# Two of the five and a half gate/up pairs of each feed-forward part as seven block products instead of eight

## The chip, the cores and the metric

The kernel runs on one core of one Trainium2 chip. The time is that of one launch on the device in microseconds (us): the median of three runs before the change is 1303.59 us, and the three lie between 1303.38 and 1304.42 us. A profile shows one execution of the same program; its times count from that execution's first instruction.

## The reference

The program is a two-layer decoder trunk over 256 tokens of width 1024, in float32. Each layer has a feed-forward part, a token mixer (differential attention in layer 0, a Mamba-2 mixer in layer 1), a cross-attention into 256 memory tokens, and a second feed-forward part. There are four feed-forward parts in all, and they are what the change touches.

```python
def swiglu(h, w_gate, w_up, w_down):
    return (jax.nn.silu(h @ w_gate) * (h @ w_up)) @ w_down
...
    h = h + 0.5 * swiglu(rmsnorm(h, ffn1_norm[i]), ffn1_w_gate[i], ffn1_w_up[i], ffn1_w_down[i])
```

Here `w_gate` and `w_up` are 1024 x 2816, and `w_down` is 2816 x 1024. The norm's root is a factor per token; it is applied after the gate/up products, its gains before them.

## The kernel before

**Tiles.** The 256 tokens are two row tiles of 128 (t = 0, 1). Width 1024 is eight tiles of 128 rows (kt = 0 to 7). The hidden width 2816 is five chunks of 512 (c = 0 to 4) and one of 256 (c = 5); a chunk of gate and of up is called a pair here. The normed activations lie transposed in `norm.x` as eight pairs of tiles (`xh`, `xl`).

**Precision by three products.** Each float32 operand is split into a high part that TensorE takes exactly and the low rest. `mm3` (L220) issues three matmuls per block: high by high (L221), high by low (L222, `wlo`) and low by high (L223, `xl`). All write 512 columns of one bank of PSUM; there are eight banks (pool `pacc`).

**Weights.** A `W` (L145) is one 1 MB tile (4 kt by 512 columns) that SP loads from device memory into pool `wp`, which has 4 buffers. A granule, `Gran` (L164), is half of it (2 kt by 512). Its `split` (L171) casts the high part on ScalarE (`whi`, L183) and subtracts on VectorE (`wlo`, L184), into pool `hp` with 4 buffers of each. `use` (L196) writes the split of a granule three granules ahead of the matmuls that take it. A cast can start when TensorE has finished the granule four places earlier, since that frees its buffer.

**A feed-forward part.** `ffn_hidden` (L572) runs `wide` (L248) over the chunks: gate 0, up 0, gate 1, up 1, and so on, each with 4 granules of 12 matmuls (2 kt x 2 row tiles x 3). After gate, ScalarE takes the silu (L581); after up, VectorE multiplies (L598); then eight transposes (`htp`, L611) and another split (L614, L615) make four of the 22 hidden tiles. Down is `out_b` (L276): half 0 of the output columns over all 22 hidden tiles, then half 1, 11 granules each. In the last part `last` does this with its own order, in which row tile 1 of half 1 goes in two pieces of 256 columns (`fin`).

**What sets the order.** The program is written with a clock of its own (`Pipe`, L108): `pipe.pe` adds the time of the matmuls written so far, and `pipe.after` puts side work (evacuations, transposes) at a later time on that clock. The scheduler of the compiler keeps that as a priority and may move an instruction on its engine when it holds it to be ready earlier. Each engine then runs its own list strictly in order.

## Time and profile before

| | |
|---|---|
| median of three runs | 1303.59 us |
| span of the profiled execution (first to last instruction) | 1301.7 us |
| TensorE (PE) busy | 1293.3 us, 99% |
| VectorE (DVE) busy | 826.3 us, 63% |
| ScalarE (ACT) busy | 716.0 us, 55% |
| GpSimd (POOL) busy | 73.1 us, 6% |
| mean rate of the DMA queues | 178 GB/s |
| granted TensorE clock, mean | 0.998 |

The profiled execution's own time is known only by its span; the median of the runs lies 1.9 us above it. In the rows, a number such as L184 is a line of the kernel before. "out<-in" names the tile that is written and those that are read. "x402 | 498.5, 1242" is the count, the busy time in us and the mean duration of one in ns. What stands behind a second bar or in brackets is the time for which the engine sat idle just before, and what ended it.

### The profile page before, as it was taken

To read this page: it belongs to the slowest core of one execution; us is meant where nothing else is said; L and a number is where in the kernel's file an instruction comes from. 1 tells how busy PE (TensorE), PEld (TensorE's weight loads), DVE (VectorE), ACT (ScalarE), POOL (GpSimd) and SP (SyncE) were. 2 spreads that over 40 slices of the span, in tenths; PEclk is the share of its full clock that TensorE was granted. 3 is DMA by queue.
4 is the path that set the end of the run, shared out by engine and by line. 5 is a ranking of instruction groups with operands and counts; after the bars stand their busy time and mean duration, and the time that the engine had idled before them with its cause. 6 is when DMAs were issued, how large, how long until landed. Compare 5 with 4: busy or idle time off the path is not lost.

```text
span 1301.7 us, 17808 instructions
## 1 busy us (share of the span) xinstructions
PE 1293.3 (99%) x6997; PEld 1112.6 (85%) x6997; DVE 826.3 (63%) x1211; ACT 716.0 (55%) x1176; POOL 73.1 (6%) x67
## 2 busy tenths in 40 slices
PE   9999999999999999999999999999999999999998
PEld 7888888788988888888888889999998998888887
DVE  5656457876666555555556446798897775655554
ACT  6456444685455545444445446677865664544432
POOL 1000002200000000000000000022132000000000
PEclk9999999999999999999999999999999999999999
DMA  9565555434445553656554655665634445655551
GB/s 329 179 220 183 188 180 193 131 129 165 161 160 162 188 190 124 226 181 212 182 186 150 211 193 185 205 195 162 195 130 168 163 157 161 208 172 172 206 178 49
DMA packets 138726, 232.01 MB, mean 178 GB/s; under 512 B 5737, under 2 KB 42258, under 8 KB 138642
## 3 DMA queue, kind: packets, MB, share of 16 engines
q1 hardware_dynamic: 137744, 229.75, 53.5%
q8 instruction: 55, 0.90, 0.3%
q10 hardware_dynamic: 738, 0.59, 0.1%
q0 software_dynamic: 160, 0.52, 0.1%
q14 instruction: 29, 0.24, 0.1%
HBM read 229.77 MB, written 1.08 MB: 177 GB/s over the span
## 4 chain that ended last, share of the span: by engine, by line
PE 96%; DVE 2%; DMA 1%; ACT 1%; issue 0%; POOL 0%; SPq 0%; POOLq 0%; ACTq 0%
PE out L221 7%; PE out L223 7%; PE out L222 7%; PE up L222 6%; PE up L223 6%; PE up L221 6%; PE gate L221 5%; PE gate L223 5%; PE gate L222 5%; PE xs L221 1%; PE htp L611 1%; PE xs L223 1%; PE xs L222 1%; PE fin L221 1%; PE fin L222 1%; PE fin L223 1%
## 5 line engine op out<-in xcount | busy, mean ns | idle before, releaser
L184 DVE TENSOR_TENSOR wlo<-w,whi 128x1024 fp32r<-128x1024 f32 (+2 forms) x446 | 526.4, 1186 | 399.6 <-ACT whi L183 398.0
L183 ACT CAST whi<-w 128x1024 fp32r<-128x1024 f32 (+1 forms) x448 | 447.6, 1006 | 463.9 <-PE out L223 141.4
L222 PE MATMUL up<-wlo,xh 128*128 128x512 f32 x320 | 124.6, 389 | 0.1
L223 PE MATMUL up<-whi,xl 128*128 128x512 f32 x320 | 124.5, 389 | 0.0
L221 PE MATMUL up<-whi,xh 128*128 128x512 f32 x320 | 124.5, 389 | 0.0
L221 PE MATMUL gate<-whi,xh 128*128 128x512 f32 x312 | 123.3, 395 | 0.0
L223 PE MATMUL gate<-whi,xl 128*128 128x512 f32 x312 | 121.7, 390 | 0.0
L222 PE MATMUL gate<-wlo,xh 128*128 128x512 f32 x312 | 121.6, 390 | 0.0
L221 PE MATMUL out<-whi,hid_hi 128*128 128x512 f32 x264 | 103.5, 392 | 0.0
L223 PE MATMUL out<-whi,hid_lo 128*128 128x512 f32 x264 | 102.8, 389 | 0.0
L222 PE MATMUL out<-wlo,hid_hi 128*128 128x512 f32 x264 | 102.7, 389 | 0.0
L222 PEld LDWEIGHTS up<-wlo,xh 128*128 128x128 f32 x320 | 60.1, 188 | 12.9 <-DVE wlo L184 0.5
L221 PEld LDWEIGHTS up<-whi,xh 128*128 128x128 f32 x320 | 60.1, 188 | 12.5
L223 PEld LDWEIGHTS up<-whi,xl 128*128 128x128 f32 x320 | 60.1, 188 | 12.5
L223 PEld LDWEIGHTS gate<-whi,xl 128*128 128x128 f32 x312 | 58.6, 188 | 12.3
L222 PEld LDWEIGHTS gate<-wlo,xh 128*128 128x128 f32 x312 | 58.7, 188 | 12.1 <-POOL wlo L184 0.4
L221 PEld LDWEIGHTS gate<-whi,xh 128*128 128x128 f32 x312 | 58.6, 188 | 11.5
L223 PEld LDWEIGHTS out<-whi,hid_lo 128*128 128x128 f32 x264 | 49.6, 188 | 10.4
L221 PEld LDWEIGHTS out<-whi,hid_hi 128*128 128x128 f32 x264 | 49.6, 188 | 10.1
L222 PEld LDWEIGHTS out<-wlo,hid_hi 128*128 128x128 f32 x264 | 49.6, 188 | 10.0
L315 POOL TENSOR_TENSOR rcol<-msq,neghalf 128x2 f32<-128x2 f32 x8 | 5.7, 718 | 683.4 <-DVE msq L313 683.4
L221 PE MATMUL fin<-whi,hid_hi 128*128 128x512 f32 (+1 forms) x110 | 38.3, 348 | 0.0
(355 smaller groups left out, 2729.9 us busy)
## 6 DMA issues: line engine op xcount, KB each, us to landing
w<-in_ffn_w_up_dram SPq DMA_DIRECT2D x40, 1024.0 KB, 5.1
w<-in_ffn_w_down_dram SPq DMA_DIRECT2D x40, 1024.0 KB, 5.2
w<-in_ffn_w_gate_dram SPq DMA_DIRECT2D x38, 1024.0 KB, 5.1
w<-in_ssd_w_in_dram SPq DMA_DIRECT2D x24, 1024.0 KB, 5.4
w<-in_xa_w_kv_dram SPq DMA_DIRECT2D x16, 1024.0 KB, 5.1
w<-in_da_w_in_dram SPq DMA_DIRECT2D x12, 1024.0 KB, 5.1
w<-in_xa_w_q_dram SPq DMA_DIRECT2D x8, 1024.0 KB, 5.1
w<-in_xa_w_o_dram SPq DMA_DIRECT2D x8, 1024.0 KB, 5.0
```

Of the source, the lines that this page charges most:

```text
L183: nc.scalar.copy(hv, src)
L184: self.eng.tensor_tensor(self.lo[:, :, o:o + n], src, hv.bitcast(F32), op=ALU.subtract)
L221: nc.tensor.matmul(o, lhsT=lh, rhs=rh, start=start, stop=False)
L222: nc.tensor.matmul(o, lhsT=lh, rhs=rl, start=False, stop=False)
L223: nc.tensor.matmul(o, lhsT=ll, rhs=rh, start=False, stop=stop)
L315: nc.gpsimd.tensor_tensor(c[:, :n], m[:, :n], neghalf[:, :n], op=ALU.pow)
L611: nc.tensor.transpose(tp[:, j, t * P:(t + 1) * P], us[t][:, (i + j) * P:(i + j + 1) * P], ident)
```

## The change

A pair is one product of a 2 x 2 by a 2 x 2 block matrix: the activations in blocks of row tile t by half h of the width (kt 0 to 3 and 4 to 7), the weights in blocks of half h by up or gate. Written out, that is eight block products of 4 kt each. For chunks 3 and 4 of each part, `seven` does it with seven products (a Strassen form) on sums of blocks:

- **Sums of activations.** `Norm.combine` adds `xh` and `xl` up to full tiles (`y`), forms four sums or differences (`sraw`), and splits them (`s_hi`, `s_lo`), once per part for both pairs. It is written to begin 8 us after the norm's last tile on the program's clock.
- **Sums of weights.** `Sum` makes x1 = b11 + b12 on VectorE into a buffer of its own; x2 = x1 + b22 and later x4 = x2 + b21 in the same buffer by DMAs that POOL issues, which read b22 and b21 once more from device memory and add them to what lies in SBUF; and x3 = b12 + b22 in place on VectorE.
- **The products.** Each product is two granules of 6 matmuls in one bank. `seven_fin` adds the seven banks up to two gate and two up tiles.
- **Order.** The 256-wide chunk comes third. Chunks 1 and 2 (the stream, 16 granules) then alternate with chunk 3's 14 granules, two and two, in a `weave`; chunk 4's 14 alternate with 14 granules of down (both halves over hidden tiles 0 to 11, 20 and 21). Half 1's partial sum is added to `h`; half 0's stays in its banks. Down then finishes over hidden tiles 12 to 19.
- **Buffers.** `wp` has 6 buffers, the small work tiles 9 for 10, and the DMA descriptors of POOL less space.

```diff
-    wp = ctx.enter_context(tc.tile_pool(name="wp", bufs=4))
+    wp = ctx.enter_context(tc.tile_pool(name="wp", bufs=6))
...
+    class Sum:
+        def __init__(self, l, r, into=None):
+            self.l, self.r, self.into, self.k0 = l, r, into, 0
+            self.t = None
+        def load(self):
+            if self.t is not None:
+                return
+            self.l.load()
+            if self.into is None:
+                self.r.load()
+                self.t = wp.tile([P, 2048], F32, name="w", tag="w").rearrange("p (k c) -> p k c", c=512)
+            else:
+                self.t = self.l.t
+            w = self.r
+            for k in (0, 2):
+                ks = slice(k, k + 2)
+                if self.into == "dma":
+                    r0 = (w.k0 + k) * P
+                    nc.gpsimd.dma_start(self.t[:, ks, :], w.src[r0:r0 + 2 * P, w.c0:w.c0 + w.n]
+                                        .rearrange("(k p) c -> p k c", p=P), accum_op=ALU.add)
+                else:
+                    nc.vector.tensor_tensor(self.t[:, ks, :], self.l.t[:, ks, :], w.t[:, ks, :], op=ALU.add)
...
+    def seven(src1, src2, c0, norm, after):
+        b11, b21 = (W(src1, k, 4, c0, 512) for k in (0, 4))
+        b12, b22 = (W(src2, k, 4, c0, 512) for k in (0, 4))
+        x1 = Sum(b11, b12)
+        x2 = Sum(x1, b22, "dma")
+        x4 = Sum(x2, b21, "dma")
+        x3 = Sum(b12, b22, "here")
+        banks = {}
+        def a(t, h):
+            return lambda k: tuple(x[:, t * P:(t + 1) * P] for x in pipe.need(norm.x, 4 * h + k))
+        def s(nm):
+            return lambda k: tuple(x[:, k * P:(k + 1) * P] for x in pipe.need(norm.s, nm))
+        plan = [(x1, s(0)), (b11, a(0, 0)), (b22, s(1)), (x2, s(2)), (b21, a(0, 1)), (x3, s(3)), (x4, a(1, 1))]
+        out = []
+        for i, (w, lhs) in enumerate(plan):
+            for k0 in (0, 2):
+                def step(g, i=i, lhs=lhs, k0=k0):
+                    if not k0:
+                        banks[i] = acc("seven")
+                    for k in range(k0, k0 + 2):
+                        lh, ll = lhs(k)
+                        mm3(banks[i], lh, ll, g.hi[:, k - k0, :], g.lo[:, k - k0, :], k == 0, k == 3)
+                        pipe.pe(0.68)
+                    if k0:
+                        if i in (0, 3):
+                            (x4 if i else x2).load()
+                        after(i, banks)
+                out.append((Gran(w.k0 + k0, 2, (w, 0, 512)), step))
+        return out
+    def weave(steps):
+        def run(*gr):
+            for g, (_, f) in zip(use(gr), steps):
+                f(g)
+        units.append(([g for g, _ in steps], run))
+    def down(src, half, ks, lhs, banks, first, last):
+        def step(g):
+            if not banks:
+                banks.extend(acc("out") for _ in range(2))
+            for k in range(g.nk):
+                kt = g.k0 + k
+                for t in range(2):
+                    xh, xl = pipe.need(lhs, kt)
+                    ts = slice(t * P, (t + 1) * P)
+                    mm3(banks[t], xh[:, ts], xl[:, ts], g.hi[:, k, :], g.lo[:, k, :], kt == first, kt == end)
+                    pipe.pe(0.68)
+                if kt == end:
+                    last(half, banks)
+        end = ks[-1][0] + ks[-1][1] - 1 if last else -1
+        return [(Gran(k, 2, (w, 0, 512)), step) for w in [W(src, k0, nk, half * 512, 512) for k0, nk in ks]
+                for k in range(w.k0, w.k0 + w.nk, 2)]
...
+            if self.mixes and len(self.x) == KT:
+                self.combine(8.0)
+        def combine(self, wait):
+            self.s = [None] * 4
+            y = [slot("y") for _ in range(4)]
+            raw = {}
+            def full(p):
+                for j in range(2):
+                    xh, xl = self.x[2 * p + j]
+                    nc.vector.tensor_tensor(v2(y[p])[:, j, :], xh.bitcast(F32), xl.bitcast(F32), op=ALU.add)
+            def part(t, h):
+                return [v2(y[2 * h + p])[:, :, t * P:(t + 1) * P] for p in range(2)]
+            def mix(i, l, r, op):
+                raw[i] = work("sraw")
+                o = raw[i].rearrange("p (h j t) -> p h j t", h=2, j=2)
+                l, r = (raw[x].rearrange("p (h j t) -> p h j t", h=2, j=2) if isinstance(x, int) else x for x in (l, r))
+                for p in range(2):
+                    lp, rp = (x[p] if isinstance(x, list) else x[:, p, :, :] for x in (l, r))
+                    nc.vector.tensor_tensor(o[:, p, :, :], lp, rp, op=op)
+            def cut(i):
+                hi, lo = slot("s_hi", F32R), slot("s_lo", F32R)
+                nc.scalar.copy(hi, raw[i])
+                nc.vector.tensor_tensor(lo, raw[i], hi.bitcast(F32), op=ALU.subtract)
+                self.s[i] = (hi, lo)
+            steps = [lambda p=p: full(p) for p in range(4)]
+            steps += [lambda: mix(0, part(1, 0), part(1, 1), ALU.subtract), lambda: cut(0),
+                     lambda: mix(2, 0, part(0, 0), ALU.subtract),
+                     lambda: mix(1, 2, part(0, 1), ALU.add), lambda: cut(1), lambda: cut(2),
+                     lambda: mix(3, part(0, 0), part(1, 0), ALU.subtract), lambda: cut(3)]
+            for i, f in enumerate(steps):
+                pipe.after(wait + 1.6 * i, f)
...
+        def seven_fin(c):
+            us, t = {}, {}
+            def after(i, b):
+                v = nc.vector
+                if i in (0, 1):
+                    t[i] = work(f"p{i}")
+                    pipe.after(0.7, lambda: nc.scalar.copy(t[i], b[i]))
+                def c12():
+                    t[3] = work("p3")
+                    v.tensor_tensor(t[3], b[3], t[1], op=ALU.add)
+                    v.tensor_tensor(t[0], t[0], t[3], op=ALU.subtract)
+                    us[0] = work("c12")
+                    v.tensor_tensor(us[0], b[2], t[0], op=ALU.add)
+                    nc.scalar.activation(us[0], us[0], AF.Silu, scale=norm.col[:, 0:1])
+                def up0():
+                    v.tensor_tensor(t[1], b[4], t[1], op=ALU.add)
+                    v.scalar_tensor_tensor(us[0], t[1], norm.col[:, 0:1], us[0], op0=ALU.mult, op1=ALU.mult)
+                def c22():
+                    us[1] = t[0]
+                    v.tensor_tensor(t[0], t[0], b[5], op=ALU.subtract)
+                    nc.scalar.activation(t[0], t[0], AF.Silu, scale=norm.col[:, 1:2])
+                    v.tensor_tensor(t[3], b[5], t[3], op=ALU.add)
+                def up1():
+                    v.tensor_tensor(t[3], b[6], t[3], op=ALU.add)
+                    v.scalar_tensor_tensor(us[1], t[3], norm.col[:, 1:2], us[1], op0=ALU.mult, op1=ALU.mult)
+                    pipe.after(T["hid"], lambda: turn(c, [us[0], us[1]], 512))
+                    extras(c)
+                if i in (3, 4, 5, 6):
+                    pipe.after(0.7, {3: c12, 4: up0, 5: c22, 6: up1}[i])
+            return after
...
         first = {} if units else dict(single=True, eng=nc.gpsimd)
-        for c in range(HID // 512):
-            wide([(wg, c * 512, 512)], norm, "gate", gate_fin(c), **first)
-            first = {}
-            wide([(wu, c * 512, 512)], norm, "up", up_fin(c))
+        wide([(wg, 0, 512)], norm, "gate", gate_fin(0), **first)
+        wide([(wu, 0, 512)], norm, "up", up_fin(0))
         c = HID // 512
         wide([(wg, c * 512, 256), (wu, c * 512, 256)], norm, "gateup", up_fin(c, 256, 256))
-        return hid
+        n = [x for c in (1, 2) for x in stream([(wg, c * 512, 512)], norm, "gate", gate_fin(c))
+             + stream([(wu, c * 512, 512)], norm, "up", up_fin(c))]
+        s = seven(wu, wg, 3 * 512, norm, seven_fin(3))
+        weave([x for i in range(0, 14, 2) for x in n[i:i + 2] + s[i:i + 2]] + n[14:])
+        s = seven(wu, wg, 4 * 512, norm, seven_fin(4))
+        wd = a[nm + "_w_down"][l]
+        banks = [], []
+        def part(half, ps):
+            def go():
+                for t in range(2):
+                    nc.vector.scalar_tensor_tensor(h[t][half], ps[t], 0.5, h[t][half], op0=ALU.mult, op1=ALU.add)
+            pipe.after(0.7, go)
+        ks = [(0, 4), (4, 4), (8, 4), (20, 2)]
+        d = down(wd, 1, ks, hid, banks[1], 0, part) + down(wd, 0, ks, hid, banks[0], 0, None)
+        weave([x for i in range(0, 14, 2) for x in s[i:i + 2] + d[i:i + 2]])
+        return hid, wd, banks[0]
     def ffn(nm, l, norm, nxt, extra=None):
-        hid = ffn_hidden(nm, l, norm, extra)
-        out_b(a[nm + "_w_down"][l], NHT, hid, upd(0.5, nxt))
+        hid, wd, bank = ffn_hidden(nm, l, norm, extra)
+        fin = upd(0.5, nxt)
+        ks = [(12, 4), (16, 4)]
+        weave(down(wd, 0, ks, hid, bank, 0, fin) + down(wd, 1, ks, hid, [], 12, fin))
...
-            cuts = [4, 4, 4, 4, 6] if half else [4, 4, 4, 4, 4, 2]
-            k0 = 0
-            for nk in cuts:
-                ws = {k: W(a["ffn2_w_down"][1], k, min(4, k0 + nk - k), half * 512, 512) for k in range(k0, k0 + nk, 4)}
+            k0 = 12
+            for nk in [2, 6] if half else [4, 4]:
+                ws = {k: W(wd, k, min(4, k0 + nk - k), half * 512, 512) for k in range(k0, k0 + nk, 4)}
...
```

The rest of the diff hands the part's state through (`hid` by index, `held` banks in `last`). What the change does to the order is shown at three places of the second feed-forward part of layer 0.

TensorE, before, where gate of a chunk gives way to its up (`gate`, `up`: the banks; `whi`, `wlo`: the split weights):

```order
L221 MATMUL gate<-whi,xh 128x512
L222 MATMUL gate<-wlo,xh 128x512
L223 MATMUL gate<-whi,xl 128x512
L221 MATMUL up<-whi,xh 128x512
L222 MATMUL up<-wlo,xh 128x512
L223 MATMUL up<-whi,xl 128x512
```

TensorE, changed, where the first product's second granule gives way to the next stream granule (`s_hi`, `s_lo`: a split sum of activations):

```order
L246 MATMUL seven<-whi,s_hi 128x512
L247 MATMUL seven<-wlo,s_hi 128x512
L248 MATMUL seven<-whi,s_lo 128x512
L246 MATMUL gate<-whi,xh 128x512
L247 MATMUL gate<-wlo,xh 128x512
L248 MATMUL gate<-whi,xl 128x512
```

Runs of 12 product matmuls now stand between runs of 24 stream matmuls, and each uses the same three-matmul block as before.

VectorE, before, at the first pairs of that part:

```order
L184 TENSOR_TENSOR wlo<-w,whi 128x1024 x7
L598 SCALAR_TENSOR_TENSOR gs<-up,rcol,gs 128x512 x2
L184 TENSOR_TENSOR wlo<-w,whi 128x1024 x2
L615 TENSOR_TENSOR hid_lo<-htp,hid_hi 128x512 x2
L184 TENSOR_TENSOR wlo<-w,whi 128x1024 x6
L598 SCALAR_TENSOR_TENSOR gs<-up,rcol,gs 128x512 x2
```

VectorE, changed, where the 256-wide chunk ends and the first weave begins (`w<-w`: the sums x1, then x3):

```order
L209 TENSOR_TENSOR wlo<-w,whi 128x2x256 x2
L187 TENSOR_TENSOR w<-w 128x1024 x2
L209 TENSOR_TENSOR wlo<-w,whi 128x1024
L794 TENSOR_TENSOR hid_lo<-htp,hid_hi 128x512 x2
L494 TENSOR_TENSOR s_lo<-sraw,s_hi 128x512
L209 TENSOR_TENSOR wlo<-w,whi 128x1024 x2
L738 SCALAR_TENSOR_TENSOR gs<-gateup,rcol,gs 128x256 x2
L209 TENSOR_TENSOR wlo<-w,whi 128x1024
L187 TENSOR_TENSOR w<-w 128x1024 x2
L794 TENSOR_TENSOR hid_lo<-htp,hid_hi 128x512
L209 TENSOR_TENSOR wlo<-w,whi 128x1024 x13
```

The sum x1 stands ahead of the weave's first split, and x3, which waits for b22, behind its fourth.

POOL, changed, over the second part of layer 0 and the first of layer 1 (each `w` row: the two halves of one accumulating DMA; before, the four `rcol` of these stages stood in one row):

```order
L416 TENSOR_TENSOR rcol<-msq,neghalf 128x2 x2
L184 DMA w<-in_ffn_w_gate_dram 128x2x512 x2
L184 DMA w<-in_ffn_w_up_dram 128x2x512 x2
L184 DMA w<-in_ffn_w_gate_dram 128x2x512 x2
L184 DMA w<-in_ffn_w_up_dram 128x2x512 x2
L416 TENSOR_TENSOR rcol<-msq,neghalf 128x2
```

Eight accumulating DMAs per part, two for each of four sums, now stand on POOL between the norms' small operations.

More of the change, by code (lines that the diff above doesn't have):

```diff
@@ L81, in work @@
     def work(name, n=512, dt=F32):
[L83 removed]
+        return wk.tile([P, n], dt, name=name, tag="v", bufs=9) if n <= 256 else wk.tile([P, n], dt, name=name, tag="w")
     ident = const.tile([P, P], F32, name="ident")
@@ L274, in wide, with stream @@
                             eng=eng if k in ((3, 5) if single else (6,)) else None) for k, nk in cut], run))
+    def stream(parts, norm, name, fin):
+        ws = [[W(src, k, 4, c0, n) for k in range(0, KT, 4)] for src, c0, n in parts]
+        ps = []
+        def step(g):
+            if not ps:
+                ps.extend(acc(name) for _ in range(2))
+            for k in range(g.nk):
+                kt = g.k0 + k
+                xh, xl = pipe.need(norm.x, kt)
+                for t in range(2):
+                    ts = slice(t * P, (t + 1) * P)
+                    mm3(ps[t], xh[:, ts], xl[:, ts], g.hi[:, k, :], g.lo[:, k, :], kt == 0, kt == KT - 1)
+                    pipe.pe(0.68)
+            if kt == KT - 1:
+                fin(ps)
+        return [(Gran(k, 2, *((w[k // 4], 0, n) for w, (_, _, n) in zip(ws, parts))), step) for k in (0, 2, 4, 6)]
@@ L1297, in run @@
                     if (t, c0) not in banks:
-                        banks[t, c0] = acc("fin")[:, :c1 - c0]
+                        banks[t, c0] = acc("fin")[:, :c1 - c0] if half else held[t]
                     b = banks[t, c0]
@@ L1302, in run @@
                             kt = g.k0 + k
-                            mms(b, t, g, k, slice(c0, c1), kt, kt == NHT - 1)
+                            mms(b, t, g, k, slice(c0, c1), kt, half == 1 and kt == 12, kt == 19)
                     if last_:
```

43 lines of the change are left out of this document (26 added, 17 removed).

## The prediction

> **What bounds the kernel now.** I read the head of the page first, then TensorE's own waits, the table of stretches, and single rows of the timeline for the pace of one matmul.
>
> ```profile
> span 1301.7 us, 17808 instructions
> PE 1293.3 (99%) x6997; PEld 1112.6 (85%) x6997; DVE 826.3 (63%) x1211; ACT 716.0 (55%) x1176; POOL 73.1 (6%) x67
> ```
>
> TensorE is busy in all but 8.4 us of the span. The waits that ended on it are few, and none lies in a feed-forward part:
>
> ```profile
> PE warm L398 <- DVE warm L99: 1.5, 1, 1.5
> PE acs L987 <- issue: 0.2, 1, 0.2
> PE qkt L673 <- POOL rt L664: 0.2, 1, 0.2
> ```
>
> One gate/up pair in the second part, and the last stretch of the span (columns: length, then busy us and count of PE, PEld, DVE, ACT, POOL, then clock, DMA share, GB/s):
>
> ```profile
> 434.00:456.66 22.66, 22.66 (x105) 18.84 (x104) 12.32 (x12) 10.76 (x12) 0.00 (x0) 1.00 0.59 187
> 1290.00:1301.70 11.70, 5.29 (x41) 4.93 (x39) 5.81 (x24) 1.82 (x4) 1.12 (x2) 0.82 0.28 91
> ```
>
> A pair keeps TensorE busy for all of 22.66 us at full clock, VectorE for 54% of it, ScalarE for 47%. Of the 8.4 idle us, 6.4 are the tail. So in the feed-forward parts the number of matmuls sets the time, and a matmul less is worth the distance from one start to the next:
>
> ```profile
> 58.67 0.39 PE L221 MATMUL gate<-whi,xh 128*128 128x512 f32 x1
> ...
> 64.79 0.39 PE L221 MATMUL gate<-whi,xh 128*128 128x512 f32 x1
> ...
> 65.25 0.39 PE L223 MATMUL gate<-whi,xl 128*128 128x512 f32 x1
> 65.47 0.39 PE L221 MATMUL up<-whi,xh 128*128 128x512 f32 x1
> ...
> 1266.98 0.28 PE L221 MATMUL fin<-whi,hid_hi 128*128 128x256 f32 x1
> ...
> 1268.89 0.28 PE L222 MATMUL fin<-wlo,hid_hi 128*128 128x256 f32 x1
> ```
>
> From 58.67 to 64.79 lie 27 starts: 0.2267 us each, not the 0.39 of one matmul's duration, which overlaps the next. The step from gate to up, into other banks, costs the same 0.22, so changing banks and operands every 6 or 12 matmuls is charged nothing. The 256-column form takes 1.91 / 16 = 0.119 us.
>
> The Trainium skill, "TensorE: Matmul & The Clock Gate", section "Back-to-back issue gap", gives a sustained roofline of about 131 ns per matmul of 512 columns. By that figure the 96 matmuls below would be worth 12.6 us; the row says 0.2267, and the row decides.
>
> **The change part by part.** *Matmuls removed.* A pair is 8 block products of 4 kt x 3 = 96 matmuls; seven make 84. Two pairs in each of four parts: 96 matmuls x 0.2267 = 21.8 us. In the last part 84 matmuls of 256 columns become 42 of 512: 84 x 0.119 - 42 x 0.2267 = 0.5 us. Transposes (176 `htp`) stay. Together 22.3 us off TensorE, which is on the path throughout.
>
> *Splits and sums added.* The durations:
>
> ```profile
> L184 DVE TENSOR_TENSOR wlo<-w,whi 128x1024 fp32r<-128x1024 f32 x402 | 498.5, 1242 | 380.8 <-ACT whi L183 379.3
> L183 ACT CAST whi<-w 128x1024 fp32r<-128x1024 f32 x402 | 421.7, 1052 | 443.9 <-PE out L223 141.4 <-PE up L223 90.0 <-PE gate L223 81.4
> L615 DVE TENSOR_TENSOR hid_lo<-htp,hid_hi 128x512 fp32r<-128x512 f32 x44 | 28.6, 683 | 3.1 <-ACT hid_hi L614 3.1
> L598 DVE SCALAR_TENSOR_TENSOR gs<-up,rcol,gs 128x512 f32<-128x512 f32 x40 | 28.2, 745 | 0.3
> L581 ACT ACTIVATE gs<-gate,rcol 128x512 f32<-128x512 f32 x40 | 27.2, 689 | 14.1 <-PE gate L223 14.0
> L614 ACT CAST hid_hi<-htp 128x512 fp32r<-128x512 f32 x44 | 24.0, 591 | 5.1 <-PE htp L611 3.5
> L1275 DVE TENSOR_TENSOR h<-h,fn 128x256 f32<-128x256 f32 x6 | 2.4, 421 | 0.0
> ```
>
> A pair had 8 granules; a seven has 14, so 48 more splits in all. I add up the first weave with its two trailing stream granules. TensorE: 16 x 12 x 0.2267 + 14 x 6 x 0.2267 + three sets of `htp` at 22.66 - 96 x 0.2267 = 0.9 each, 65.3 us. VectorE: 30 splits x 1.242 = 37.3; four weight sums of the same shape, 5.0; nine operations of `seven_fin`, 7 x 0.683 + 2 x 0.745 = 6.3; four up products, 3.0; six `hid_lo`, 4.1. That is 55.7 us, 85% of TensorE's time where it was 54%. ScalarE: 30 x 1.052 + 2 copies and 6 `hid_hi` x 0.591 + 6 silus x 0.689 = 40.4, 62%. On the sum VectorE still fits; it could hold TensorE up only where work bunches. A weight sum does so twice per weave.
>
> The steady rhythm of the kernel before shows the reserve:
>
> ```profile
> 548.04 1.05 ACT L183 CAST whi<-w 128x1024 fp32r<-128x1024 f32 x1 [1.67 <-PE out L223]
> 549.13 1.23 DVE L184 TENSOR_TENSOR wlo<-w,whi 128x1024 fp32r<-128x1024 f32 x1 [1.50 <-ACT whi L183]
> ```
>
> A cast starts when TensorE ends the granule four back, and `wlo` is done 2.3 us later (548.04 to 550.36). TensorE wants it after the three granules between: 3 x 2.72 = 8.2 us before, reserve 5.8. A seven granule lasts 6 x 0.2267 = 1.36, so three in a row last 5.4 us at least (two of 1.36, one of 2.72), reserve 3.1, about two more operations of 1.24 on VectorE.
>
> *The tight place: x3.* x3's sum stands on VectorE behind the weave's fourth split, and needs b22. Six buffers hold the sum, b11, b12 and three stream tiles, so b22 takes the first stream tile's, free after the second split. Rows for that:
>
> ```profile
> w<-in_ffn_w_up_dram SPq DMA_DIRECT2D x40, 1024.0 KB, 5.1
> SPq L161 <- DVE wlo L184: 933.4, 182, 11.2
> 62.76 0.37 SPq L161 DMA_DIRECT2D w<-in_ffn_w_up_dram  x1
> ```
>
> SP indeed waits for `wlo` to give buffers back. From the second split's end to the fourth's are two granules of TensorE, 5.4 us; issue and landing take 0.4 + 5.1 = 5.5. So VectorE may wait 0.1 us, and then do x3 (2 x 1.24), a `hid_lo` (0.68) and the fifth split (1.24). From TensorE's start of the weave that is 2.3 + 0.1 + 2.5 + 0.7 + 1.2 = 6.8 us, and the fifth granule is wanted at 2 x 2.72 + 2 x 1.36 = 8.2. Reserve 1.4 us, four times in the run. Behind the waiting sum stand the splits of all later granules; TensorE waits for them. A landing up to 1.4 us late is free; the longest that I allow, 3 us late, costs 1.5 us per part. Bounds 0 to 6 us, and I take 0.5, nearer the median row. The second weave's x3 has the same distance and one down granule more between.
>
> *The activation sums.* Per part 16 operations of 128x256 and four of 128x512 on VectorE (16 x 0.42 + 4 x 0.68 = 9.5 us) and four casts on ScalarE. They lie beside gate 0, up 0 and the 256-wide chunk, 3 x 10.9 us of TensorE in which a pair's rows leave VectorE 46% free, 15 us. Bounds 0 to 1.5 us per part (one split late), value 0.2, since nothing needs them before the weave. In the first part rope tables (some 25 small operations) lie in a weave too: 0 to 2 us, value 0.2.
>
> *The accumulating DMAs.* x2 and x4, 16 sums of 1 MB. The run before has no such DMA. Their cover: x1's second split ends 2.3 us after TensorE starts the weave, and x2's first cast comes when TensorE has ended the weave's 11th granule, 6 x 2.72 + 5 x 1.36 = 23.1 us after that start. Cover 20.8 us; the same for x4. Below, a plain 1 MB load takes 5.1 us; above, reading and rewriting the tile as separate passes makes 10.2 to 15.3. All are inside, so no cost. I take 10.2, the one that counts both operands read. POOL's issue is small:
>
> ```profile
> L1246 POOL DMA_DIRECT2D fn<-in_vec_dram x2 | 1.3, 647 | 0.0
> L664 POOL TENSOR_TENSOR rt<-rt,rt 128x512 f32<-128x512 f32 x8 | 14.0, 1750 | 42.4 <-DVE rt L663 36.8 <-issue 5.6
> ```
>
> The rotary sums (L664) lie outside the feed-forward parts, and an `rcol` comes before or after a part's eight DMAs, so nothing urgent queues behind them. The traffic:
>
> ```profile
> GB/s 329 179 220 183 188 180 193 131 129 165 161 160 162 188 190 124 226 181 212 182 186 150 211 193 185 205 195 162 195 130 168 163 157 161 208 172 172 206 178 49
> DMA packets 138726, 232.01 MB, mean 178 GB/s; under 512 B 5737, under 2 KB 42258, under 8 KB 138642
> ```
>
> 16 MB are added to 232. The first weave moves 8 MB of stream, 4 of blocks and 2 of sums in 65 us, 215 GB/s; the first slice shows that 329 can be had.
>
> The Trainium skill, "Collectives: The Full Stack", section "The bandwidth ceiling: the fold count and why AG ≠ RS ≠ AR", says that an adding transfer runs at half rate because it reads two sources, not because the add costs anything. By that a sum takes an estimated 10.2 us and the total stays; no run so far shows it.
>
> *Buffers and tail.* Deeper prefetch is worth nothing where TensorE does not wait. The last unit still has 6 kt, so the tail keeps its 6.4 us.
>
> Sum for the profiled execution: 1301.7 - 22.3 + 0.5 + 0.2 x 4 + 0.2 = 1280.9 us; the median of the runs lies 1.9 above the span, 1282.8. I allow 0.7 more for bunching that I have not placed: **1283.5 us**, 20 us or 1.5% faster.
>
> **The rivals.** *VectorE sets the weaves (0.17).* For it: 85% over 65 us, and its list is strictly in order, with waits for ScalarE, TensorE's banks and loads in it. Against it: reserves of 1.4 and 3.1 us. If each of the eight weaves lost one split (1.24) and a little waiting, 1.5 us, it would be 12 us: 1293.5.
>
> *The accumulating DMA is late (0.06), slower.* The place is ScalarE's cast of x2 and x4, with every later split behind it. The price is 16 x (T - 20.8) us for a time T per sum. From T = 20.8 + 22.3 / 16 = 22.2 us the change loses. At five plain loads, 25.5 us, it would be 1303.6 - 22.3 + 75 = 1356. For it: no row shows such a DMA, and POOL's operations vary (L664 averages 1750 ns). Against it: four plain loads fit into the cover.
>
> *It does not do what it says (0.05), same.* If the weave's matmuls did not keep 0.2267 us (more waits per matmul, short runs in a bank), 1.5% more on each of the roughly 6800 would use the gain up: about 1303. Against it is the step from gate to up.
>
> **How the numbers follow.** The forecast, nearly all of the removed matmul time seen, has 0.72: 1281 (no stall at all, 1303.6 - 22.3 = 1281.3) to 1288 (the bounds of x3's and the activation sums about half used). The range 1280.5 to 1294 takes in the VectorE rival; what it leaves out is the late DMA, the case of no gain, and a little beyond. A measurement of this kernel tells about 0.2% (2.6 us) from no change. Faster: 0.72 + 0.17 = 0.89; same 0.05; slower 0.06.
>
> **What would show it.** Right: some 140 fewer matmuls at 0.227 us, TensorE still at 99%, VectorE near 85% in the weaves, the accumulating DMAs landing in well under 20.8 us. Wrong: TensorE waits for `wlo` in the weave's first ten microseconds (x3), many short ones all along (VectorE), or ScalarE's cast waits for a DMA from POOL. A pace other than 0.227 us would refute the first term.

## The result

The changed kernel takes **1280.76 us**, median of four runs (1280.60 to 1281.74), against 1303.49 (1303.35 to 1304.42) for the kernel before, measured beside it: ratio 0.9826, 95% interval 0.9812 to 0.984. That is 22.7 us or 1.74% faster, well over the 0.2% that can be told here. The forecast was 1283.5 in a range of 1280.5 to 1294, faster with 0.89. The profiled execution took 1280.77 us, 1.8 more than its span.

The head of the page of the changed kernel:

```profile
span 1279.0 us, 17993 instructions
PE 1269.5 (99%) x6859; PEld 1091.3 (85%) x6859; DVE 980.9 (77%) x1435; ACT 782.0 (61%) x1256; POOL 111.9 (9%) x99
```

There are 138 matmuls fewer (96 removed, 42 for 84 in the last part), and TensorE is busy as before in all but 9.5 us of the span. VectorE went from 63% to 77%. The two longest waits that ended on TensorE (in us: total, times, longest):

```profile
PE warm L538 <- DVE warm L99: 1.5, 1, 1.5
PE gate L288 <- ACT whi L208: 1.1, 1, 1.1
```

Both are at the very start: the first before the warm-up matmuls (`warm`), the second on the first weights. Two more, of 0.2 us each, lie outside the feed-forward parts, so none is in a weave. Where the time went is read from two landmarks that the change does not touch: the last start of the rotary transposes (`qkt`, behind the first feed-forward part) and of the state products (`py`, behind the third). The views of these tiles give count, shortest/median/longest ns, first and last start; of the kernel before:

```profile
L673 PE MATMUL qkt<-ident,rt x32: 270/273/328, 220.7 to 257.4; 128*128 128x128 f32 x32
L1156 PE MATMUL py<-xd,E x128: 217/275/275, 859.6 to 991.8; 128*128 128x64 f32 x128
```

and of the changed one:

```profile
L868 PE MATMUL qkt<-ident,rt x32: 270/273/327, 215.0 to 251.7; 128*128 128x128 f32 x32
L1351 PE MATMUL py<-xd,E x128: 217/275/275, 843.0 to 975.2; 128*128 128x64 f32 x128
```

The first part gave 257.4 - 251.7 = 5.7 us, the second and third together 16.6 - 5.7 = 10.9, the last 22.7 - 16.6 = 6.1. The 24 matmuls of a part are worth 24 x 0.2267 = 5.44, and the last has 0.5 more for its wider form. The shares fit to 0.3 us each.

The two weaves of the second part, from the first matmul of each to the first one behind it, in the table of stretches (length; busy us and count of PE, PEld, DVE, ACT, POOL; clock; DMA share; GB/s):

```profile
442.78:507.65 64.87, 64.87 (x298) 53.87 (x296) 51.29 (x52) 38.94 (x43) 7.26 (x6) 1.00 0.79 227
507.65:566.59 58.94, 58.94 (x270) 48.96 (x268) 45.41 (x47) 34.23 (x37) 2.43 (x2) 1.00 0.80 249
```

The first lasts 64.87 us, all of it TensorE. The prediction added up 65.3 with three sets of `htp` (24 transposes); 20 of them, two and a half sets, lie in the weave. VectorE is busy for 51.3 us, 79%, and 45.4, 77%.

### The profile page after: what moved, and what is told of

The parts are those of the page before. It is cut to its first block, busy times and chain, and to the rows that moved or that the text cites. A ratio compares the mean times of both kernels' runs of the same rounds, so it can differ in the third digit from the quotient of the medians.

```text
span 1279.0 us, 17993 instructions
## 1 busy us (share of the span) xinstructions
PE 1269.5 (99%) x6859; PEld 1091.3 (85%) x6859; DVE 980.9 (77%) x1435; ACT 782.0 (61%) x1256; POOL 111.9 (9%) x99
## 2 busy tenths in 40 slices
DMA packets 147449, 248.80 MB, mean 195 GB/s; under 512 B 6266, under 2 KB 42787, under 8 KB 147363
## 4 chain that ended last, share of the span: by engine, by line
PE 96%; DVE 2%; ACT 1%; DMA 1%; issue 0%; POOL 0%; POOLq 0%; ACTq 0%
PE out L248 9%; PE out L246 9%; PE out L247 9%; PE seven L248 4%; PE seven L247 4%; PE seven L246 4%; PE up L247 3%; PE up L248 3%; PE up L246 3%; PE gate L248 3%; PE gate L246 3%; PE gate L247 3%; PE xs L246 2%; PE htp L790 2%; PE xs L248 1%; PE xs L247 1%
## 5 line engine op out<-in xcount | busy, mean ns | idle before, releaser
L209 DVE TENSOR_TENSOR wlo<-w,whi 128x1024 fp32r<-128x1024 f32 (+1 forms) x494 | 582.5, 1186 | 221.8 <-ACT whi L208 213.9
L208 ACT CAST whi<-w 128x1024 fp32r<-128x1024 f32 (+2 forms) x496 | 497.7, 1011 | 354.2 <-PE out L248 129.9
L247 PE MATMUL up<-wlo,xh 128*128 128x512 f32 x192 | 74.8, 390 | 0.1
L248 PE MATMUL up<-whi,xl 128*128 128x512 f32 x192 | 74.7, 389 | 0.0
L247 PEld LDWEIGHTS out<-wlo,hid_hi 128*128 128x128 f32 x336 | 63.2, 188 | 12.6
L246 PE MATMUL gate<-whi,xh 128*128 128x512 f32 x184 | 72.7, 395 | 0.0
L248 PE MATMUL gate<-whi,xl 128*128 128x512 f32 x184 | 71.8, 390 | 0.0
L247 PE MATMUL gate<-wlo,xh 128*128 128x512 f32 x184 | 71.7, 390 | 0.0
L246 PE MATMUL seven<-whi,s_hi 128*128 128x512 f32 x128 | 49.8, 389 | 0.0
L247 PE MATMUL seven<-wlo,s_hi 128*128 128x512 f32 x128 | 49.8, 389 | 0.0
L248 PE MATMUL seven<-whi,s_lo 128*128 128x512 f32 x128 | 49.8, 389 | 0.0
```

The lines of the kernel that those rows point to most:

```text
L208: nc.scalar.copy(hv, src)
L209: self.eng.tensor_tensor(self.lo[:, :, o:o + n], src, hv.bitcast(F32), op=ALU.subtract)
L246: nc.tensor.matmul(o, lhsT=lh, rhs=rh, start=start, stop=False)
L247: nc.tensor.matmul(o, lhsT=lh, rhs=rl, start=False, stop=False)
L248: nc.tensor.matmul(o, lhsT=ll, rhs=rh, start=False, stop=stop)
```

## The experiments

The theory throughout is that the count of matmuls sets the time and everything that the change added is hidden. The rivals were that the new order brought the gain, that VectorE or the adding DMAs are nearly late, and that the buffers matter. After that came the question of how far the same step can be carried.

**The new order with eight products.**

```diff
-        s = seven(wu, wg, 3 * 512, norm, seven_fin(3))
-        weave([x for i in range(0, 14, 2) for x in n[i:i + 2] + s[i:i + 2]] + n[14:])
-        s = seven(wu, wg, 4 * 512, norm, seven_fin(4))
+        def pair(c):
+            return stream([(wg, c * 512, 512)], norm, "gate", gate_fin(c)) + stream([(wu, c * 512, 512)], norm, "up", up_fin(c))
+        s = pair(3)
+        weave([x for i in range(8) for x in n[2 * i:2 * i + 2] + s[i:i + 1]])
+        s = pair(4)
...
-        weave([x for i in range(0, 14, 2) for x in s[i:i + 2] + d[i:i + 2]])
+        weave([x for i in range(7) for x in s[i:i + 1] + d[2 * i:2 * i + 2]] + s[7:])
```

The norms form no sums of activations there (`mixes=False`).

> The changed kernel's order and buffers (granules in turn, six weight buffers, the last gate/up pair among down granules), but all pairs by 8 block products, so no weight sums, no activation sums and no adding DMAs. Theory COUNT (the time went because 24 matmuls per part went, and nothing else): the 96 matmuls come back and only the 42 for 84 of the last part (0.5 us) and a start 0.3 us earlier stay, so 1302.7 us (1302.0 to 1303.6). Rival ORDER (the new order or the deeper buffers bring part of the gain, and the sums cost part of a larger one): a third or more of the 22.7 us stays, 1296 or less; or, if the order alone costs, above 1304.5.

Measured: 1302.73 us (1302.31 to 1303.90), ratio 0.9993 (0.9983 to 1.0002).

```profile
PE 1292.2 (99%) x6955; PEld 1110.1 (85%) x6955; DVE 830.2 (64%) x1219; ACT 716.1 (55%) x1176; POOL 72.7 (6%) x67
```

The order, the deeper buffers and the turn of gate/up and down granules are worth nothing that can be told. From this kernel to the changed one, with 96 matmuls fewer in the same order, the median falls by 22.0 us. The two were measured on two occasions, each beside the kernel before; by the two ratios it is 21.8 us, 0.227 per matmul. The count theory stands.

**x2 and x4 on VectorE, no adding DMA.**

```diff
-        x2 = Sum(x1, b22, "dma")
-        x4 = Sum(x2, b21, "dma")
+        x2 = Sum(x1, b22, "here")
+        x4 = Sum(x2, b21, "here")
@@ Sum.load
+                if self.into == "here":
+                    self.r.load()
@@ seven
-                        if i in (0, 3):
-                            (x4 if i else x2).load()
+                        if i in (1, 4):
+                            (x4 if i > 1 else x2).load()
```

> The changed kernel with x2 and x4 made on VectorE too (four more operations of 1.2 us per pair, 38 us in all) instead of by adding DMAs. VectorE's load in the second part's two weaves rises from 51.7 of 65.3 us and 45.4 of 58.9 to about 56.5 (87%) and 50.2 (85%). Theory RESERVE (VectorE may run some 3 us late before TensorE sees it, and a sum of two operations, 2.4 us, fits): 1280.8 to 1282. Rival VECTORE (bunching decides before the mean does): each of the 16 added sums costs 0.5 to 1 us, 1289 to 1297, with TensorE waiting for wlo in the weaves.

Measured: 1281.15 us (1280.38 to 1282.16), ratio 0.9826 (0.981 to 0.9843), the same as the change. The two weaves of the second part in the table of stretches:

```profile
444.18:509.05 64.87, 64.87 (x297) 53.85 (x296) 55.34 (x56) 38.95 (x43) 0.00 (x0) 1.00 0.56 188
509.05:567.99 58.94, 58.94 (x269) 48.97 (x268) 49.77 (x51) 34.24 (x37) 0.00 (x0) 1.00 0.63 219
```

VectorE at 85% with two more sums per pair still holds nothing up: both weaves last as long as in the changed kernel. So the reserve is real and larger than the change uses, and at two pairs the adding DMAs save VectorE work that nobody waited for: without them the DMA engines are busy 56% instead of 79% of the first weave.

**Five weight buffers for six.**

```diff
-    wp = ctx.enter_context(tc.tile_pool(name="wp", bufs=6))
+    wp = ctx.enter_context(tc.tile_pool(name="wp", bufs=5))
```

> The changed kernel with five weight buffers for six. The scheduler places x3's sums later on VectorE for it, and SyncE's loads come one buffer later. Theory of the prediction (deeper prefetch is worth nothing where TensorE does not wait, but b22 takes a buffer that must come free in time): a load issued one tile later, up to 5.4 us, with 5.1 to land, still finds most splits' tiles in place; x3's sums, placed later, cost at most a few us in all: 1281 to 1286. Rival BUFFERS: the two more buffers of the change are what makes the weaves run without a stall; x1, b11, b12 and b22 leave one for the stream, whose next tile then lands 3 us or more too late twice per weave: 16 x 3 us, and the same again by a lower clock after each stall, 1330 or more.

Measured: 1280.88 us (1280.57 to 1281.89), no difference. The sixth buffer is worth nothing; the scheduler put x3's sums behind more splits instead (in the second part at 456.81, where the changed kernel has them at 445.57).

**The adding DMA held back, by one and by two products.** A VectorE operation on one column, which multiplies an element of the product's bank by zero and adds it to the tile, makes the DMA wait. The diff is that for one product; for two, (2, 5) and 5 stand for (1, 4) and 4.

```diff
+                    tie = self.t[:, k, 0:1]
+                    nc.vector.scalar_tensor_tensor(tie, bank[:, 0:1], 0.0, tie, op0=ALU.mult, op1=ALU.add)
                     nc.gpsimd.dma_start(self.t[:, ks, :], ..., accum_op=ALU.add)
@@ seven
-                        if i in (0, 3):
-                            (x4 if i else x2).load()
+                        if i in (1, 4):
+                            (x4 if i == 4 else x2).load(banks[i])
```

> The changed kernel with each adding DMA held back until the block product after next-door has ended: x2's starts when the second product is done, x4's when the fifth is, by a tiny VectorE operation that reads that product's bank and adds nothing to the tile. That shortens the cover to some 6.8 us before ScalarE could cast the tile, 11.3 us before TensorE would stand still (6.8 + 1.4 + 5.4 - 2.3 for cast and wlo). Theory LANDING (512 KB need 1.2 us of POOL and 6.1 to 7.0 to land, so the cast is at most 1.5 us late): 1280.8 to 1283. Rival SLOW ADD (the two halves of one sum really need 15 us or more, which the long cover of the changed kernel hides): 4 us or more per sum, 1345 or more.

> As the run with the adding DMA held back by one product, but by two: x2's starts when the third product is done, x4's when the sixth is. Nothing is left of the cover on ScalarE's side, and TensorE has two companion granules, 5.4 us, before it wants the sum. Theory LANDING: 0.3 for the tie, 1.2 for the issue, 6.2 to land, 2.3 for cast and wlo make 10.0 us, so each of 16 sums costs 4.6 us, and the second half, 1.2 us later, nothing more: about 1354 us (1335 to 1375), with ScalarE's cast waiting for a DMA of POOL. Rival HIDDEN ANYWAY (other work moves up and fills the hole): under 1300.

Measured, one execution each: 1311.30 and 1387.53 us. Both came out dearer than the LANDING theory: 30.5 us where none to two were expected, 107 where 73 were, 1.9 and 6.7 us per sum. Held back by two products, the first sum of the second part shows why. TensorE in the timeline (start, length, in brackets the idle time before it and who ended it), then the table of stretches:

```profile
502.04 0.39 PE L250 MATMUL up<-whi,xl 128*128 128x512 f32 x1
505.54 0.76 PE L248 MATMUL seven<-whi,s_hi 128*128 128x512 f32 x1 [3.12 <-ACT whi L210]
506.80 0.80 PE L249 MATMUL seven<-wlo,s_hi 128*128 128x512 f32 x1 [0.50 <-DVE wlo L211]
...
507.82 0.63 PE L248 MATMUL seven<-whi,s_hi 128*128 128x512 f32 x1
508.25 0.63 PE L249 MATMUL seven<-wlo,s_hi 128*128 128x512 f32 x1
```

```profile
502.00:506.00 4.00, 0.89 (x3) 0.26 (x2) 0.48 (x1) 1.04 (x1) 0.00 (x0) 0.95 1.11 202
506.00:510.00 4.00, 3.50 (x9) 2.28 (x9) 3.02 (x4) 2.68 (x3) 0.00 (x0) 0.50 0.06 10
510.00:514.00 4.00, 4.00 (x18) 3.33 (x17) 3.68 (x4) 2.29 (x4) 0.00 (x0) 0.70 0.11 16
514.00:518.00 4.00, 4.00 (x19) 3.27 (x19) 3.51 (x5) 2.00 (x3) 0.00 (x0) 1.00 0.70 250
```

The stall itself is 3.6 us, less than the 4.6 expected, since TensorE starts again with `whi` alone. But then the granted clock is 0.50, from 505.61 to 512.44 by the table of stretches, and matmuls start 0.43 us apart instead of 0.2267. The head of its page:

```profile
span 1385.5 us, 18042 instructions
PE 1310.8 (95%) x6859; PEld 1110.7 (80%) x6859; DVE 981.1 (71%) x1467; ACT 775.9 (56%) x1256; POOL 112.4 (8%) x99
```

Over the run TensorE's idle time rose from 9.5 to 74.7 us, 4.1 per sum, and its busy time, with the same matmuls, by 41.3, 2.6 per sum. The mean clock fell from 0.999 to 0.972, and 0.027 of 1385.5 us is 37 of these 41. On average a stall here cost 1.6 times itself. By the clock in the same table, 14 of the 16 stalls (the waits for `whi` of a sum, 2.2 to 5.0 us) were followed by 3.41 or 6.83 us at 0.50; two of 2.2 us were not. The Trainium skill, "TensorE: Matmul & The Clock Gate", section "What's actually happening", has the clock fall to half after an idle window of about 3.4 us and return after a busy one as long. The rows agree with the half and with the length of the slow stretches, one or two such windows; but the clock also fell after stalls of 2.3 us here and of 1.8 us in the run held back by one product, so 3.4 us without a matmul are not needed for it.

Held back by one product, the stalls are short (the longest 1.8 us) but the landing is not what was expected. Median us from issue to landing, and the stretch around the first such sum of the second part:

```profile
w<-in_ffn_w_gate_dram POOLq DMA_DIRECT2D x16, 512.0 KB, 10.2
w<-in_ffn_w_up_dram POOLq DMA_DIRECT2D x16, 512.0 KB, 7.7
```

```profile
467.00:482.00 15.00, 15.00 (x68) 12.23 (x66) 6.51 (x8) 5.57 (x7) 2.49 (x2) 1.00 0.94 257
```

Two stream loads of 1 MB went out at 467.45 and 469.86, beside the two halves of the sum at 468.4 and 469.7, and the DMA engines were 94% busy. The first half was cast at 477.11, the second at 481.24. In the changed kernel no load went out between 439.93 and 451.25, and the halves of the same sum at 442.97 and 446.01. So the landing time of a sum depends on what is issued beside it: 6.1 and 7.0 us (medians of the gate and the up rows) in the changed kernel, 10.2 and 7.7 here. Of the 30 us, 16.0 are more idle time of TensorE, and after two of the stalls the clock was 0.50 for 10.2 us together; the rest was not taken apart.

**A plain DMA for the adding one.**

```diff
-                                        .rearrange("(k p) c -> p k c", p=P), accum_op=ALU.add)
+                                        .rearrange("(k p) c -> p k c", p=P))
```

> The changed kernel with the 32 adding DMAs of 512 KB turned into plain ones from the same places to the same places by the same queue: x2 and x4 then hold b22 and b21 alone, so the addition is left out of what is computed. Theory HALF RATE (an adding transfer takes about twice a plain one, since it reads the tile as well): these land in 3.1 to 4.0 us where they took 6.1 and 7.0. Rival QUEUE (the queue of GpSimd, or the loads beside, set the landing): still 5.5 to 7 us. The time stays at 1280.8 either way.

Measured: 1281.4 us in one execution, and in the list of issues:

```profile
w<-in_ffn_w_gate_dram POOLq DMA_DIRECT2D x16, 512.0 KB, 4.9
w<-in_ffn_w_up_dram POOLq DMA_DIRECT2D x16, 512.0 KB, 5.2
```

The changed kernel has 6.1 and 7.0 in these rows. Adding costs 1.2 to 1.8 us per half, of which 0.48 is GpSimd's issue (1.204 us against 0.724, by the view of the tile). For the landing neither theory is right: the ratio is 1.24 to 1.35. The half rate that the prediction took from the Trainium skill, "Collectives: The Full Stack", section "The bandwidth ceiling: the fold count and why AG ≠ RS ≠ AR", does not show in the landing of a 512 KB sum. It does show in the time for which the DMA engines are held. The queue of GpSimd in the changed kernel and here (packets, MB, share of 16 engines' span):

```profile
q0 software_dynamic: 8864, 17.30, 7.7%
```

```profile
q0 software_dynamic: 4768, 17.30, 3.9%
```

For the same bytes the adding transfers take twice as much of the engines' time.

**A third pair by seven products.** The one pair left and the 256-wide chunk go in among the products.

```diff
-        wide([(wg, c * 512, 256), (wu, c * 512, 256)], norm, "gateup", up_fin(c, 256, 256))
...
+        n = stream([(wg, c * 512, 256), (wu, c * 512, 256)], norm, "gateup", up_fin(c, 256, 256))
+        n += stream([(wg, 512, 512)], norm, "gate", gate_fin(1)) + stream([(wu, 512, 512)], norm, "up", up_fin(1))
+        s = [x for c in (2, 3, 4) for x in seven(wu, wg, c * 512, norm, seven_fin(c))]
...
+        n += d
+        cut = [round(i * len(n) / 21) for i in range(22)]
+        weave([x for i in range(21) for x in n[cut[i]:cut[i + 1]] + s[2 * i:2 * i + 2]])
```

> A third gate/up pair per part (columns 1024 to 1535) by 7 products: 42 granules of the three pairs in turn with 26 others (the 256-wide chunk, the one pair left, the first 14 down granules), two by one. TensorE per part loses 12 more matmuls, 4 x 12 x 0.2267 = 10.9 us. VectorE in that stretch by the prediction's durations: 68 splits x 1.242 + 12 weight sums x 1.24 + 3 x 6.3 + 9 hid_lo x 0.68 + 4 ups x 0.745 + 4 x 0.68 = 130 us against TensorE's 132; the two weaves of the changed kernel came to 0.93 of such a sum, so 121 us, 92%. Theory COUNT: 1280.8 - 10.9 = 1269.9 us (to 1272). Rival VECTORE: at 92%, and with 24 sums of 2.4 us in a rhythm of 5.44 us in which three splits and the pair's own operations already take 4.5, each sum costs up to 1.2 us, 1285 to 1299, with TensorE waiting for wlo throughout.

Measured: 1283.66 us (1283.29 to 1284.17), ratio 0.9844 (0.9829 to 0.9858): 2.9 us worse than two pairs, 13.8 off the count. But not as the VectorE rival has it. The weave of the second part, then three stretches of the first and the cast that ended its long stall:

```profile
439.01:571.23 132.22, 132.22 (x602) 109.51 (x600) 116.40 (x124) 85.57 (x97) 13.32 (x11) 1.00 0.89 263
```

```profile
34.00:38.00 4.00, 3.65 (x19) 2.51 (x18) 4.00 (x9) 3.54 (x5) 1.37 (x1) 1.00 0.19 24
...
42.00:46.00 4.00, 0.82 (x4) 0.34 (x2) 3.83 (x6) 0.62 (x1) 0.00 (x0) 1.00 1.09 291
46.00:50.00 4.00, 3.31 (x8) 2.67 (x9) 1.81 (x3) 2.44 (x5) 0.00 (x0) 0.57 1.04 386
```

```profile
46.02 1.14 ACT L208 CAST whi<-w 128x512 fp32r<-128x512 f32 x2 [2.54 <-DMA w<-in_ffn_w_up_dram]
```

In the second part TensorE is busy throughout, for 132.2 us where 132 were expected, with VectorE at 88%. In the first part it stands still from 42.82 to 46.69, on the cast of a load that is late, and again the clock falls. The load went out only at 39.60: SP had waited 14.2 us for a `wlo` that frees a buffer, and from 34 to 38 us the DMA engines were 19% busy. So the load was late because its buffer came free late; the full DMA engines came only after that. By the landmarks (last `qkt` at 259.8, last `py` at 978.8) the first part lost 10.8 us against the count, the next two together 1.0, the last 2.3. The stall and the slower clock behind it are some 5.5 of the 10.8; the rest was not taken apart.

**The same with x1 and x3 summed on GpSimd.** `nc.gpsimd.tensor_tensor` for `nc.vector.tensor_tensor` in `Sum.load`.

> The three-pair kernel with the weight sums x1 and x3 on GpSimd instead of VectorE. VectorE falls by 15 us per part, to some 107 of 132 us (81%, as in the changed kernel's weaves). GpSimd's sums are slower (its 128x512 sums L859 take 1.1 to 2.3 us, so 2.3 to 4.6 for 128x1024) and it also issues the adding DMAs, 1.2 us each, behind them. Theory COUNT: 1269.9 (to 1272) if the sums come in time. Rival GPSIMD LATE: x1's sum is wanted two granules after its second block has landed, and if two operations of 4.6 us stand there, some 4 us per pair are lost, 12 pairs: 1318 or more, TensorE waiting for whi of a sum.

Measured: 1318.74 us (1313.25 to 1320.64), slower than the kernel before (1.0106, 1.0083 to 1.0128). That is the time of the GPSIMD LATE rival, but not its mechanism: the sums take 2.9 us each, below the 4.6 feared, and TensorE waits longest for VectorE's `p`, not for `whi` of a sum. What went wrong stands in the timeline; GpSimd's row, then VectorE's in the same time:

```profile
438.19 6.21 POOL L187 TENSOR_TENSOR w<-w 128x1024 f32<-128x1024 f32 x2 [5.04 <-DVE wlo L209]
```

```profile
439.50 2.63 DVE L209 TENSOR_TENSOR wlo<-w,whi 128x1024 fp32r<-128x1024 f32 x1 [0.72 <-ACT whi L208]
442.05 2.90 DVE L494 TENSOR_TENSOR s_lo<-sraw,s_hi 128x512 fp32r<-128x512 f32 x1
```

TensorE's longest wait, and the same two engines at one of its five times:

```profile
PE htp L790 <- DVE p L778: 16.2, 5, 5.5
```

```profile
500.11 5.26 POOL L187 TENSOR_TENSOR w<-w 128x1024 f32<-128x1024 f32 x2
```

```profile
500.65 5.28 DVE L778 SCALAR_TENSOR_TENSOR p<-p,rcol,p 128x512 f32<-128x512 f32 x1
```

While GpSimd adds, VectorE's split takes 2.63 us instead of 1.22, the `s_lo` 2.90 instead of 0.68, and the `p` 5.28 instead of 0.74. VectorE's busy time over the run rose from 1039.3 to 1067.3 us, though 58.5 us of sums were gone from it. The Trainium skill, "SBUF — State Buffer", section "🔬 SBUF: two separate sides", says that VectorE and GpSimd share a pair of ports as a lock for a whole instruction, also where a VectorE operation has two SBUF inputs and GpSimd reads SBUF. The rows agree: GpSimd's two sums end at 444.40, and the `s_lo` that began beside the second of them ends at 444.95.

**Three pairs where the loads are ahead.** One kernel has three pairs in the last three parts and two in the first; one has three everywhere, with the first part's 256-wide chunk ahead of the products as in the changed kernel:

```diff
+        if first:
+            wide([(wg, c * 512, 256), (wu, c * 512, 256)], norm, "gateup", up_fin(c, 256, 256))
+        else:
+            n += stream([(wg, c * 512, 256), (wu, c * 512, 256)], norm, "gateup", up_fin(c, 256, 256))
```

> Three pairs by 7 products in the second, third and fourth part, two (as in the changed kernel) in the first. In the run with three pairs everywhere, TensorE lost its 12 matmuls' 2.7 us per part and gave back 10.7 us in the first part (weights still on their way, activation sums, rope tables), 1.0 in the second and third together, 2.3 in the last. Theory PLACE (three pairs fit wherever the loads are ahead, the first part was the whole trouble): 1280.8 - 3 x 2.7 + 1.0 + 2.3 = 1275.9 us (1274.5 to 1277.5). Rival VECTORE (at over 90% the stalls come back elsewhere, now that the parts start in another phase): 1279 or more.

> Three pairs in every part, but in the first part the 256-wide chunk stands ahead of the products, as in the changed kernel, so that the first sum's blocks have 10.9 us more to land. Theory PLACE: the first part then loses 2.7 us less or more of its stall: 1273.2 if none is left, up to 1276. Rival: the first part's rope tables and activation sums, not the loads, are what made VectorE late there, and 5 us or more of the stall stay, 1278 or more.

Measured: 1276.28 us (1275.35 to 1276.75), ratio 0.9789 (0.9774 to 0.9803); and **1274.18 us** (1273.79 to 1274.37), ratio 0.9773 (0.9759 to 0.9788). Both as the PLACE theory has it. The second is the fastest kernel here, 6.6 us below the change. Its largest waits on TensorE:

```profile
PE warm L538 <- DVE warm L99: 1.5, 1, 1.5
PE htp L790 <- DVE p L778: 1.2, 2, 0.6
```

Of the count's 10.9 us 4.3 are still missing. TensorE's idle time, 10.4 us for 9.5 in the changed kernel, is 0.9 of them; the rest is in its busy time, and its cause stays open. Moving the 256-wide chunk gave the loads more time and VectorE too, so this run alone does not part the two.

**x3 by an adding DMA as well**, `x3 = Sum(b12, b22, "dma")`, in each of these two:

> As the run with three pairs in the last three parts, with x3's sum too by an adding DMA in place of VectorE (11 pairs x 2.4 us off VectorE, 11 MB more through the DMA queues, in weaves that move 260 GB/s already). Theory VECTORE (what is left of the stalls is VectorE's load): 2 to 3 us faster than that run, 1273 to 1274. Rival TRAFFIC (the queues are 0.93 busy in stretches of that weave, so loads and sums land later): 3 us or more slower than that run, and again the lower clock after each stall.

> Three pairs in every part with the 256-wide chunk first in the first part, and x3's sum too by an adding DMA. With three pairs in the last three parts alone that brought 1.0 us (1276.28 to 1275.26). The count's bound is 1280.8 - 10.9 = 1269.9, and 1274.2 was reached with x3 on VectorE, so 4.3 us are left. If VectorE's load is what they are: 1272.7 to 1273.5. If the fuller queues (more than 260 GB/s) take it back, as the first part is where the loads are shortest of time: 1274.2 or more.

Measured: 1275.26 us (1274.81 to 1275.80) and 1276.48 (1275.34 to 1276.81): 1.0 us better in the first, where the runs of the two kernels overlap, and 2.3 worse in the second, where they do not. The first is neither theory's figure, the second is that of fuller queues. The first part's stretch of the kernel with three pairs everywhere, with x3 on VectorE and then by DMA:

```profile
30.00:165.00 135.00, 134.67 (x612) 110.97 (x611) 128.26 (x179) 95.44 (x118) 15.44 (x13) 1.00 0.88 261
```

```profile
30.00:165.00 135.00, 133.37 (x606) 110.02 (x605) 120.77 (x170) 92.83 (x116) 22.73 (x19) 1.00 0.97 281
```

VectorE falls from 95% to 89%, and the DMA engines rise from 88% to 97% busy: the load is moved from one resource that is nearly full to another. The landmark behind the first part comes 1.8 us later (252.2 for 250.4), where the two profiled executions differ by 1.2 us, so the loss is in the first part.

## Why the prediction was right

*The matmul term* (-22.3 us) is the whole result. The landmarks give 22.7, and the order with eight products gives back all but about 1 us of it. The pace held, also across changes of bank and operand. First matmuls of two block products and of the stream granules between them in the changed kernel:

```profile
448.71 0.39 PE L246 MATMUL seven<-whi,s_hi 128*128 128x512 f32 x1
...
456.87 0.39 PE L246 MATMUL seven<-whi,xh 128*128 128x512 f32 x1
```

There are 36 starts in 8.16 us, 0.2267 each, with two changes in them. The rival of a lost pace is refuted, and so is the 131 ns per matmul from the Trainium skill, "TensorE: Matmul & The Clock Gate", section "Back-to-back issue gap", which gave 12.6 us. Of the 0.4 us beyond the sum most came in the first 20 us. The first `up` matmul, before and after:

```profile
19.48 0.39 PE L221 MATMUL up<-whi,xh 128*128 128x512 f32 x1
```

```profile
19.18 0.39 PE L246 MATMUL up<-whi,xh 128*128 128x512 f32 x1
```

*VectorE's load* was put at 85% and measured 79%. The sum took 1.242 us per operation; in a row they overlap a little (two sums in 2.35 us). It also counted six `hid_lo`, of which three lie in the weave (2.0 us for 4.1). At 85%, with the sums of x2 and x4 on it, VectorE still cost nothing, and at 88% in the weave of three pairs TensorE did not wait either. So the rival that VectorE sets the weaves was given more chance (0.17) than it had, since the reserves work: a sum delays the splits for one or two granules and they catch up.

*The tight place, x3*, came out as worked out, partly by luck. VectorE and then TensorE in the timeline of the first weave:

```profile
444.42 1.23 DVE L209 TENSOR_TENSOR wlo<-w,whi 128x1024 fp32r<-128x1024 f32 x1 [0.45 <-ACT whi L208]
445.57 2.35 DVE L187 TENSOR_TENSOR w<-w 128x1024 f32<-128x1024 f32 x2
447.84 0.68 DVE L794 TENSOR_TENSOR hid_lo<-htp,hid_hi 128x512 fp32r<-128x512 f32 x1
448.44 1.22 DVE L209 TENSOR_TENSOR wlo<-w,whi 128x1024 fp32r<-128x1024 f32 x1
```

```profile
442.78 0.39 PE L246 MATMUL gate<-whi,xh 128*128 128x512 f32 x1
...
451.66 0.39 PE L247 MATMUL gate<-wlo,xh 128*128 128x512 f32 x1
```

x3 followed its split without a wait: b22 was there. The fifth split was done at 449.66, 6.9 us after TensorE began the weave (predicted 6.8). Two errors made that agree: the fourth split ended 2.9 us after the start instead of 2.3, and what stood behind it took 4.0 us instead of 4.5, as operations overlap and x3 did not wait. `wlo` was used at 451.66, a reserve of 2.0 us where 1.4 was forecast: four `htp` in between added 0.5, and `wlo` is only the second matmul of its granule (0.2). The 0.5 us for x3, 0.8 for the activation sums of four parts, 0.2 for the rope tables and 0.7 for bunching, 2.2 us in all, did not come; with the 0.4 us above they are why 1280.8 was measured and 1283.5 forecast. So every allowance turned out at nothing, and the time lies only 0.3 us above the lower end of the range. No run showed a cost of the activation sums at two pairs.

*The adding DMAs* had a cover of 20.8 us by the prediction. In the changed kernel:

```profile
442.97 1.24 POOL L184 DMA_DIRECT2D w<-in_ffn_w_gate_dram  x1 [30.62 <-DVE wlo L209]
446.01 1.20 POOL L184 DMA_DIRECT2D w<-in_ffn_w_gate_dram  x1 [1.80 <-DVE wlo L209]
```

```profile
466.59 1.06 ACT L208 CAST whi<-w 128x1024 fp32r<-128x1024 f32 x1 [0.30 <-PE seven L248]
467.95 1.06 ACT L208 CAST whi<-w 128x1024 fp32r<-128x1024 f32 x1 [0.30 <-PE seven L248]
```

The halves go out at 442.97 and 446.01, and are cast at 466.59 and 467.95: covers of 23.6 and 21.9 us against 6 to 7 to land. No cost, as said. The price that the rival put on lateness, 16 x (T - 20.8), left out the clock: held back by two products a sum cost 4.1 us of idle time and 2.6 more of slower work. It also took T for a fixed time, and the landing turned out to depend on the loads beside it.

*Buffers worth nothing*: five gave the same time as six. *Traffic*: 227 GB/s for the predicted 215, with no wait on it. The sum took a tile for 1 MB; one of 1024 KB is 1.05 (over the run 248.80 MB for 232.01, 16.8 more for 16 sums), which gives 225.

## What to carry to other kernels

Where one engine is busy for 99% and its instructions keep a steady distance, removing instructions is worth their count times that distance, and the added work is priced by the reserve of each engine in the stretch where it lands, not by its share of the whole run: here VectorE could go to 88% there without a cost. Moving work to a second resource helps only if that resource does not share something with the first: GpSimd took VectorE's time with it, and x3's sums by DMA brought no clear gain in one kernel and cost 2.3 us in the other, where the DMA engines were 97% busy in the first part. A stall of TensorE should be priced with the slower clock that can follow it: stalls of 2.2 to 5.0 us cost 1.6 times their length on average here.

## What the runs showed of the hardware

- After a stall of 3.6 us TensorE's granted clock was 0.50 for 6.83 us, and matmuls started 0.43 us apart. Of 16 stalls of 2.2 to 5.0 us 14 were followed by such a stretch, of 3.41 or 6.83 us, and the mean clock fell to 0.972. A stall of 1.8 us could do it, too.
- VectorE operations with two SBUF inputs took 2.63 us (for 1.22) and 2.90 (for 0.68) while GpSimd ran 128x1024 sums of about 2.9 us, and one took 5.28 (for 0.74) beside two of them.
- An adding DMA of 512 KB from GpSimd landed in 6.1 to 7.0 us where a plain one of the same queue took 4.9 to 5.2; beside two 1 MB loads the median rose to 10.2. Its issue took 1.20 us of GpSimd, the plain one's 0.72, and for the same bytes it took twice as much of the DMA engines' time (7.7% of the span for 3.9%).
- Weight sums by DMA brought nothing over VectorE at two pairs: 1280.76 and 1281.15 us.
